# A two-layer decoder trunk on one core: one projection's banks, the order of the recurrence's output, late gating operands, and the final norm under the last product

## The chip, the core and the metric

The kernel runs on one core of a Trainium2 chip. The metric is the time of one execution on the device in microseconds (us). The core has a matmul engine (TensorE, PE in the profile), three engines for elementwise work (VectorE, DVE; ScalarE, ACT; GpSimd, POOL) and SyncE (SP), which here only starts DMAs. Each engine takes its own instructions in order and waits at semaphores for the others. PE writes its products into PSUM, which has eight banks of 128 x 512 f32. All else lies in SBUF.

## What is computed

512 tokens of width 1024 go through two layers; each adds to x half an FFN, a mixer, and half another FFN, all of normed x. The mixer of layer 0 is a recurrence, that of layer 1 a gated spatial mixer (gMLP). A final norm ends it.

```python
def rms_norm(x, g):
    y = xf * lax.rsqrt(jnp.mean(xf * xf, axis=-1, keepdims=True) + NORM_EPS)
    return (y * g.astype(jnp.float32)).astype(x.dtype)

def swiglu(x, w_in, w_out):                 # w_in 1024 x 5632, w_out 2816 x 1024
    g, u = jnp.split(x @ w_in, 2, axis=-1)
    return (jax.nn.silu(g) * u) @ w_out

def recurrent_mixer(...):
    y, r = jnp.split(x @ w_in, 2, axis=-1)
    y = jax.nn.gelu(y)
    r = causal_depthwise_conv(r, conv_w, conv_b)
    h = rg_lru(r, gate_a_w, gate_a_b, gate_x_w, gate_x_b, lam)
    return (y * h) @ w_out

def spatial_gating_mixer(...):
    u, v = jnp.split(jax.nn.gelu(x @ w_in), 2, axis=-1)
    v = rms_norm(v, v_norm)
    ...
    return (u * sg) @ w_out                 # sg: v mixed over positions, by head

for i in range(DEPTH):
    h = h + 0.5 * swiglu(rms_norm(h, ffn1_norm[i]), ffn1_w_in[i], ffn1_w_out[i])
    hn = rms_norm(h, mix_norm[i])
    ...
    h = h + m
    h = h + 0.5 * swiglu(rms_norm(h, ffn2_norm[i]), ffn2_w_in[i], ffn2_w_out[i])
return rms_norm(h, final_norm)
```

## The kernel before

**Steps.** The whole program is one list of steps (`subs`), each a block of weights of 256 x 512 and the matmuls that use it, mostly twelve of 128 x 512. The loop at the end of `trunk` goes through the list: for step i it issues what is hooked to i as "pre", then the splitting of the weights of step i + 3 (`SPLIT_AHEAD`), then the hooks "mid" and "rest", new loads, the matmuls of step i, and the hooks "end" and "late". `hook(n, phase, fn)` is how everything else (copies out of PSUM, transposes, norms, sums) gets its place. The order on every engine is so written out by hand.

**Splitting.** Each f32 operand is held as the sum of two fp32r parts. For a weight block ACT makes `whi` (line 96) and DVE makes `wlo` = raw - whi (line 87); for the left operand, `hi` and `lo`. A product takes three matmuls: hi with whi (line 360), lo with whi (line 361), hi with wlo (line 362). Four buffers each hold whi and wlo.

**Seven products.** `seven` computes a 2 x 2 block product of halves (tokens by columns, summed over two halves of the inner dimension) with seven products in place of eight, by Winograd's sums. The products are P1, P2, P5, P6, P3, P7, Q4, each over one or two groups (`cuts`, `ci` is the group). Their left operands are blocks A11, A12, A22, A21 of the left matrix and its sums S1 = A21 - A22, S2 = S1 - A11, S4, S3 (`s1`, `s2`, `s4`, `s3` on DVE); their right operands are weight blocks W11, W12, W21, W22 and sums of these. A weight sum comes about in one of two ways: an accumulating load on POOL's queue (`Raw.add`, line 136, "plus" or "then"), or a DVE add of two raw blocks (`Sub.add`, the group raw<-raw,raw of line 87). P6's operand is made in the second way, from P5's block and a tile of W22, which P3 then uses again. Results lie in PSUM under the names A (P1, then P6, P7, Q4 added to it), B (P2), C (P5, then P3), and Q (a bank of its own for Q4 in output products).

**Banks.** Six banks are for products (`bank`), two are aux banks (`aux`), in which PE transposes the left operands (tile e, line 264).

**The four places that the change touches.**
1. *First FFN chunk.* The first step list of all is a pair product (`pair_plain`, tile p, line 714) with four banks; `post` computes h = silu(p) * p with ACT and DVE (line 93), which frees its banks. Then a `chunk` follows through `seven`: P1 into A, P2 into B, P5 into C and so on; `p2` adds B to the copy c1 on DVE. h is transposed by `left_blocks` (tile e).
2. *The recurrence's output.* `recurrent` computes y in eight steps; the first three y are copied out of PSUM by DVE (`drain`, COPY y<-r), gelu follows on ACT, and DVE computes the scans and y * h, whose blocks are the left operands of the output product in `out_blocks`, in the order P1 P2 P5 of each group, then P6 P6 P3 P3 P7 P7 Q4 Q4.
3. *The norm before the spatial mixer* (`BlockNorm` with `plain`). x is transposed and multiplied by the gain; A21 is also split straight from PSUM (`direct`: per group twice ACT hi and DVE lo). Two transposes of the position weights (`tr_ws`, `take_ws`, tile wst) are hooked beside the mixer's first product.
4. *The final FFN's output and the final norm* (`FinalNorm`). Products in the usual order with Q4 last; for Q4 the first group's matmuls are held back and run with the second's (`joined`). Tokens lie in four tiles; tiles 0 and 1 get their last part from P3, tiles 2 and 3 from Q4. For each tile ACT squares and sums the two halves, ACT takes the root, DVE corrects the reciprocal by one Newton step (`newton`), and the two halves are multiplied by it and the gain on DVE and ACT and stored, one DMA on SP's queue and one on ACT's.

```python
def seven(block, cuts, left, w, posts, order=None, own=False, apart=False, joined=None):
    ...
    if fresh and ci == 0:
        for s in range(2):
            bk[name, s] = bank(name)[:, :w]
```

Of the kernel before, what the change touches and what calls it, by code (L numbers as in the profile page):

```python
# [13 lines left out]
P = 128  # L14
# [38 lines left out]
def trunk(ctx: ExitStack, tc: tile.TileContext, a: dict, out: bass.AP):  # L53
# [191 lines left out]
    class Group:  # L245
# [46 lines left out]

        def stage(self, n, name, src, gains=None, parts=True, where=None, direct=False):

            st = {}
            hook(n, "end", lambda: st.update(ps=self.turn(src, where)))
            first = name == "A21"
            hook(n + 1, "pre" if first else "mid", lambda: self.take(name, st["ps"], gains))
            if direct:
                hook(n + 1, "mid", lambda: self.direct(name, st["ps"], gains))  # L300
            hook(n + 1, "mid", st.clear)
            if parts:
                hook(n + 1, "mid", lambda: self.parts("S1" if first else name))
# [28 lines left out]

    def seven(block, cuts, left, w, posts, order=None, own=False, apart=False, joined=None):

# [7 lines left out]
        def mm_of(prod, ci):  # L342
# [102 lines left out]
    class BlockNorm:  # L445
# [102 lines left out]
    def out_blocks(w, k0, groups, scale, norm=None, order=None, own=False):  # L548
# [36 lines left out]

        def p3(s, ps):
            upd(s, 1, ps, scale)
            final(s, 1, "A12", s)
# [6 lines left out]
        def q4(s, ps):  # L595
            if hasattr(norm, "last"):
                norm.last(2 + s, ps, scale)
                return
            upd(2 + s, 0, ps, scale)
            final(2 + s, 0, "A21", s)  # L600

        at0 = len(subs)
# [39 lines left out]

    def chunk(w_in, f0, nt, group):

# [34 lines left out]
        def q4(s, ps):  # L679
# [4 lines left out]
            if s == 1:  # L684
                left_blocks(group, ht, 1)

        seven(in_block(w_in, lambda n: n * DFF + f0 * P, w), [[0, 1], [2, 3]], x_left(), w,
              dict(P1=p1, P2=p2, P5=p5, P6=p6, P3=p3, P7=p7, Q4=q4))

    def pair_plain(w_in, f0, group, first=False):  # L690
# [14 lines left out]
        def product(sub, half, left, h, between=None):  # L705

            sq = [(s, q) for q in range(2) for s in range(2)]
            for i, (s, q, m) in enumerate([(s, q, m) for m in range(3) for s, q in sq] if first and h else
                                          [(s, q, m) for q in range(2) for m in range(3) for s in range(2)] if first else
                                          [(s, q, m) for s, q in sorted(sq) for m in range(3)]):  # L710
                if i == 8 and between is not None:
# [4 lines left out]
                                 stop=left[2] == "1" and (h, q, m) == (1, 1, 2))  # L716

        def post(half):
            for s in range(2):
                ps, t = st[half, s], 2 * half + s  # L720
                s1, o = slot(name="s1")[:, :w], slot(name="h")[:, :w]
                act(s1, ps[:, :w], AF.Silu, scale=S.rt[:, t : t + 1])
                stt(o, ps[:, w:], S.rt[:, t : t + 1], s1, ALU.mult, ALU.mult)
# [31 lines left out]
    def ffn(w_in, w_out, norm):  # L755
        f0 = 0
        for i, sizes in enumerate(FF_PARTS):
            groups, p0 = [], f0
            for n in sizes:
# [11 lines left out]

    class FinalNorm:
        def __init__(self):
            self.gain, self.ms, self.r = {}, {}, {}

# [5 lines left out]

        def mean(self, t, n):

            junk = slot(name="junk")
            q = cp.tile([P, 1], F32, tag=f"ssq{t}{n}", name=f"ssq{t}{n}")
            act(junk, xt(t, n), AF.Square, accum_out=q)
            m = cp.tile([P, 1], F32, tag=f"ms{t}{n}", name=f"ms{t}{n}")
            ts(m, q, 1.0 / D, self.ms.get(t, EPS), ALU.mult, ALU.add)
            self.ms[t] = m

        def root(self, t):
            self.r[t] = tiny(1)
            act(self.r[t], self.ms[t], AF.Sqrt)

        def newton(self, t):
            r, m, c = self.r[t], self.ms[t], tiny(1)
# [8 lines left out]
        def store(self, t):  # L805

            o = xt(t, 0)
            stt(o, o, self.r[t], self.gain[0], ALU.mult, ALU.mult)
            act(xt(t, 1), xt(t, 1), AF.Copy, scale=self.r[t])
            for n, q in ((0, nc.sync), (1, nc.scalar)):  # L810
                q.dma_start(out=out[0, t * P : (t + 1) * P, n * 512 : (n + 1) * 512], in_=xt(t, n))

        def piece(self, t, n):
            at = now[0]
            if t < 2:
                hook(at + 1, "pre" if n == 1 else "mid", lambda: self.mean(t, n))
                if n == 1:
                    hook(at + 1, "mid", lambda: self.root(t))
                    hook(at + 2, "pre", lambda: self.newton(t))
                    hook(at + 2, "rest", lambda: self.grown(t, 1))  # L820
                    hook(at + 3, "rest", lambda: self.store(t))
            else:
                self.mean(t, n)
                hook(at + 1, "rest", lambda: self.grown(t, 1))

        def last(self, t, ps, scale):
            stt(xt(t, 0), ps, scale, xt(t, 0), ALU.mult, ALU.add)
            if t == 3:
                self.store(2)
            self.mean(t, 0)  # L830
            self.root(t)
            self.newton(t)
            if t == 3:
                self.store(3)


    def recurrent(w_in, w_out, norm):
# [83 lines left out]

        def drain(c):
            y = slot(name="y")
            nc.vector.tensor_copy(y, ym[c])
            ym[c] = y

        def gelu(c):
# [89 lines left out]
    def spatial(w_in, w_out, norm):  # L1017
# [256 lines left out]
    ffn(a["ffn2_w_in"][1], a["ffn2_w_out"][1], last)  # L1274
    hook(len(subs) - 24, "late", last.load)


# [153 lines left out]
```

## Time and profile before

| | |
|---|---|
| median of 3 runs | 1650.31 us (1649.54 to 1651.78) |
| the profiled execution's own time | 1652.41 us |
| its span in the trace | 1650.7 us, granted TensorE clock 0.992 |
| last matmul ends | 1637.40 us from the span's start |
| accumulating loads on POOL, issue to landing | medians 7.6 (ffn_w_in) and 8.0 us (ffn_w_out), 5.9 us (rec_w_out) |

Times below are counted from the start of the span. In the waits view a line names the waiting engine, tile and line, what released it, and the total, number and longest of such waits in us. In a timeline each row has start, duration, engine, line, operation and tiles, and in brackets the idle time before it with its releaser. Matmuls are pipelined: each takes 0.39 us by its row, but a 128 x 512 one starts 0.227 us after the one before it. The same holds on DVE and ACT in a smaller measure (a wlo takes 1.22 us and the next instruction starts 1.14 after it).

### The profile page before, as it was taken

The page shows a single profiled execution, that of the slowest core. Times are in us where ns is not written, and L with a number is a line of the kernel's source. Part 1 is how long each engine was busy: PE and PEld are TensorE (multiplying, and loading weights), DVE is VectorE, ACT ScalarE, POOL GpSimd, SP SyncE. Part 2 cuts the span into 40 slices and gives each one's busy share as a digit, 9 for nine tenths or more (in the row PEclk, how much of TensorE's full clock was granted, in tenths as well). Part 3 has the DMA queues.
Part 4 walks back from the last instruction along what each step waited for, and adds up shares of the span by engine and source line. Part 5 has one row for each costly group of instructions (what it writes and reads, how often), then busy time and mean ns, then how long its engine had stood idle before and what let it go on. Part 6 is the DMA issues. An engine that isn't in the chain of part 4 may idle for free.

```text
span 1650.7 us, 20821 instructions
## 1 busy us (share of the span) xinstructions
PE 1621.5 (98%) x7475; PEld 1336.7 (81%) x7475; DVE 1367.8 (83%) x1836; ACT 1032.8 (63%) x1498; POOL 210.7 (13%) x191
## 2 busy tenths in 40 slices
PE   8999999999999999999999999999999999999996
PEld 6788888888878888888888888888788888888885
DVE  6898898887898787978887978778866888879777
ACT  6656656657866656556775565566864865665655
POOL 1111111100000111111101111112100011121110
PEclk9999999999999999999999999999999999999999
DMA  5767876943363786866838768768753557696682
GB/s 212 161 170 173 204 170 163 212 132 96 101 168 86 175 199 160 212 170 159 207 86 181 187 172 209 167 161 225 183 158 90 152 120 186 166 211 166 158 205 77
DMA packets 160744, 271.97 MB, mean 165 GB/s; under 512 B 11280, under 2 KB 37504, under 8 KB 160640
## 3 DMA queue, kind: packets, MB, share of 16 engines
q1 hardware_dynamic: 113424, 181.95, 35.3%
q0 software_dynamic: 44992, 86.06, 31.3%
q10 hardware_dynamic: 2224, 2.63, 0.5%
q8 instruction: 59, 0.97, 0.2%
q14 instruction: 45, 0.37, 0.1%
HBM read 268.50 MB, written 2.10 MB: 164 GB/s over the span
## 4 chain that ended last, share of the span: by engine, by line
PE 88%; DVE 7%; ACT 3%; issue 1%; DMA 0%; SPq 0%; ACTq 0%; DVEq 0%
PE A L361 13%; PE A L360 13%; PE A L362 13%; PE C L361 7%; PE C L362 7%; PE C L360 7%; PE p L714 4%; PE B L360 3%; PE B L362 3%; PE B L361 3%; PE e L264 3%; DVE wlo L87 2%; PE Q L360 1%; PE Q L362 1%; PE Q L361 1%
## 5 line engine op out<-in xcount | busy, mean ns | idle before, releaser
L96 ACT ACTIVATE whi<-raw 128x1024 fp32r<-128x1024 f32 (+1 forms) x530 | 546.9, 1033 | 407.9 <-PE A L361 111.9
L87 DVE TENSOR_TENSOR wlo<-raw,whi 128x1024 fp32r<-128x1024 f32 (+1 forms) x531 | 631.2, 1191 | 198.8 <-ACT whi L96 197.7
L360 PE MATMUL A<-whi,hi 128*128 128x512 f32 x984 | 392.7, 399 | 0.8 <-DVE x L93 0.8
L361 PE MATMUL A<-whi,lo 128*128 128x512 f32 x984 | 385.5, 392 | 4.8 <-DVE lo L87 4.8
L362 PE MATMUL A<-wlo,hi 128*128 128x512 f32 x984 | 385.8, 392 | 0.0
L361 PEld LDWEIGHTS A<-whi,lo 128*128 128x128 f32 x984 | 186.0, 189 | 42.8 <-DVE lo L87 5.8
L362 PEld LDWEIGHTS A<-wlo,hi 128*128 128x128 f32 x984 | 185.6, 189 | 40.3
L360 PEld LDWEIGHTS A<-whi,hi 128*128 128x128 f32 x984 | 185.6, 189 | 38.2 <-ACT hi L96 1.6
L361 PE MATMUL C<-whi,lo 128*128 128x512 f32 x544 | 212.4, 390 | 1.4 <-DVE lo L87 1.2
L360 PE MATMUL C<-whi,hi 128*128 128x512 f32 x544 | 212.3, 390 | 0.0
L362 PE MATMUL C<-wlo,hi 128*128 128x512 f32 x544 | 211.8, 389 | 0.0
L136 POOL DMA_DIRECT2D raw<-in_ffn_w_in_dram x80 | 96.4, 1205 | 753.4 <-DVE raw L87 560.8
L136 POOL DMA_DIRECT2D raw<-in_ffn_w_out_dram x72 | 83.0, 1153 | 387.3 <-DVE wlo L87 153.5
L87 DVE TENSOR_TENSOR raw<-raw,raw 128x1024 f32<-128x1024 f32 (+1 forms) x110 | 131.9, 1199 | 0.5
L87 DVE TENSOR_TENSOR lo<-a,hi 128x512 fp32r<-128x512 f32 (+1 forms) x188 | 122.5, 658 | 3.9 <-ACT hi L96 3.4
L361 PEld LDWEIGHTS C<-whi,lo 128*128 128x128 f32 x544 | 102.1, 188 | 24.7 <-DVE lo L87 3.7
L96 ACT ACTIVATE hi<-a 128x512 fp32r<-128x512 f32 (+1 forms) x188 | 112.5, 600 | 14.3 <-DVE a L87 12.1
L362 PEld LDWEIGHTS C<-wlo,hi 128*128 128x128 f32 x544 | 102.1, 188 | 21.2
L360 PEld LDWEIGHTS C<-whi,hi 128*128 128x128 f32 x544 | 102.1, 188 | 21.0
L360 PE MATMUL B<-whi,hi 128*128 128x512 f32 x272 | 110.2, 405 | 5.3 <-DVE h L93 5.3
L96 ACT ACTIVATE c<-A 128x512 f32<-128x512 f32 x126 | 74.3, 595 | 57.6 <-PE A L362 57.1
L361 PE MATMUL B<-whi,lo 128*128 128x512 f32 x272 | 107.0, 393 | 0.0
(168 smaller groups left out, 2206.9 us busy)
## 6 DMA issues: line engine op xcount, KB each, us to landing
raw<-in_ffn_w_in_dram SPq DMA_DIRECT2D x160, 512.0 KB, 4.5
raw<-in_ffn_w_out_dram SPq DMA_DIRECT2D x100, 512.0 KB, 5.6
raw<-in_ffn_w_in_dram POOLq DMA_DIRECT2D x80, 512.0 KB, 7.6
raw<-in_ffn_w_out_dram POOLq DMA_DIRECT2D x60, 512.0 KB, 8.0
raw<-in_sg_w_in_dram SPq DMA_DIRECT2D x18, 512.0 KB, 5.3
raw<-in_rec_w_in_dram SPq DMA_DIRECT2D x16, 512.0 KB, 3.8
raw<-in_ffn_w_in_dram SPq DMA_DIRECT2D x30, 256.0 KB, 3.8
raw<-in_ffn_w_out_dram SPq DMA_DIRECT2D x20, 256.0 KB, 5.3
```

Source lines behind the costliest of these rows:

```text
L87: nc.vector.tensor_tensor(out=o, in0=x, in1=y, op=op)
L96: nc.scalar.activation(out=o, in_=x, func=f, **k)
L136: nc.gpsimd.dma_start(out=self.v, in_=src, accum_op=ALU.add)
L264: nc.tensor.transpose(ps[:, o : o + P], src(q, s), ident)
L360: nc.tensor.matmul(ps, zh, wh, start=fresh and i == 0, stop=False, **k)
L361: nc.tensor.matmul(ps, zl, wh, start=False, stop=False, **k)
L362: nc.tensor.matmul(ps, zh, wl, start=False, stop=end, **k)
L714: nc.tensor.matmul(bank_of(half, s), z, (sub.lo if m == 2 else sub.hi)[:, q, :], start=left[2] == "2" and (h, q, m) == (0, 0, 0), stop=lef ...
```

## The change

By place:

1. In the first FFN, the first chunk's B takes the two aux banks (`spare`). The pair's silu is hooked one step earlier and split from the rest of `post`; h's transposes are hooked two steps later (`left_blocks` with 4 for 2).
2. In the recurrence's output the order becomes P1 P5 P2 for each group, then P6 P3 for each, then P7 P7 Q4 Q4. The three copies of y are removed; gelu reads PSUM. Where P5 and P6 of a group are at least four steps apart (`far`), P6's weight sum is made by a second accumulating load onto P5's block, and P3 loads its own W22. By its distance this also holds for the first group in the spatial mixer's output. The sums s2, s4, s3 get other hooks.
3. In the plain norm `direct` of A21 runs five steps later, and the position weights' transposes and copies two steps later.
4. In the final FFN's output the order ends with P3, which is held back in the place of Q4, so that tiles 2 and 3 are finished first. `FinalNorm` is rewritten: half of the factor is put into the gain beforehand, the square's scale holds 1/1024, the root takes its bias from the other half's sum, the Newton step works on two tiles at once where it can, ACT's root table is loaded ten steps before the end, and the eight stores go out singly, seven on SP's queue and one on ACT's.

```diff
-        def stage(self, n, name, src, gains=None, parts=True, where=None, direct=False):
+        def stage(self, n, name, src, gains=None, parts=True, where=None, direct=0):
...
             if direct:
-                hook(n + 1, "mid", lambda: self.direct(name, st["ps"], gains))
-            hook(n + 1, "mid", st.clear)
+                hook(n + direct, "mid", lambda: self.direct(name, st["ps"], gains))
+            hook(n + max(direct, 1), "mid", st.clear)
...
-                        bk[name, s] = bank(name)[:, :w]
+                        bk[name, s] = (spare if name == "B" else bank)(name)[:, :w]
...
+        def far(ci):
+            return own and order.index(("P6", ci)) - order.index(("P5", ci)) >= 4
...
                 if own:
                     raw[11, ci] = new(0, 0, (0, 1))
+                    if far(ci):
+                        then = block(1, 1, cuts[ci])
...
+            elif prod == "P6" and far(ci):
+                r, then = raw[11, ci], block(1, 0, cuts[ci])
...
-                r = raw[22, ci]
+                r = new(1, 1) if far(ci) else raw[22, ci]
...
-                        self.plain if name == "A21" else name != "A22", direct=name == "A21")
+                        self.plain if name == "A21" else name != "A22",
+                        direct=0 if name != "A21" else 6 if self.plain else 1)
...
         def p3(s, ps):
+            if ends:
+                norm.last(s, ps, scale)
+                return
...
-                      "Q4" if hasattr(norm, "last") else None)
+                      "P3" if ends else None)
...
-                lead = 4 if isinstance(norm, TileNorm) and prod in ("P7", "Q4") else 3 if 1 in n else 2
+                lead = 6 if ends and prod == "P3" else 4 if isinstance(norm, TileNorm) and prod in ("P7", "Q4") else 3 if 1 in n else 2
...
+        def silu(half, s):
+            t = 2 * half + s
+            ht[t] = slot(name="s1")[:, :w]
+            act(ht[t], st[half, s][:, :w], AF.Silu, scale=S.rt[:, t : t + 1])
...
-            left_blocks(group, ht, half, 2)
+            left_blocks(group, ht, half, 4 if first else 2)
...
-                    end = (lambda: hook(at0 + 8, "rest", lambda: post(0))) if first else lambda: post(0)
+                    end = (lambda: (hook(at0 + 7, "rest", lambda: (silu(0, 0), silu(0, 1))),
+                                    hook(at0 + 8, "mid", lambda: post(0)))) if first else lambda: post(0)
...
-                    chunk(w_in, f0, n, groups[-1])
+                    chunk(w_in, f0, n, groups[-1], aux if len(subs) == 8 else bank)
...
+        ORDER = [(p, ci) for p in ("P1", "P2", "P5", "P6", "P7", "Q4", "P3") for ci in range(2)]
...
+        def root(self, t, n):
...
+            act(self.s[g][:, i : i + 1], self.q[g, n][:, i : i + 1], AF.Sqrt, bias=self.m[g][:, i : i + 1])
+
+        def newton(self, g, n, i):
+
+            r, q, m = self.s[g][:, i], self.q[g, n][:, i], self.m[g][:, i]
+            w = i.stop - i.start
+            v, c = tiny(w), tiny(w)
+            tt(v, q, m, ALU.add)
             nc.vector.reciprocal(out=r, in_=r)
-            stt(c, m, r, r, ALU.mult, ALU.mult)
-            ts(c, c, -0.5, 1.5, ALU.mult, ALU.add)
-            tt(r, r, c, ALU.mult)
+            if w == 1:
+                stt(c, r, v, r, ALU.mult, ALU.mult)
+            else:
+                tt(c, r, r, ALU.mult)
+                tt(c, c, v, ALU.mult)
+            stt(r, c, -3.0, r, ALU.add, ALU.mult)
...
+        def last(self, t, ps, scale):
+            stt(xt(t, 1), ps, scale, xt(t, 1), ALU.mult, ALU.add)
+            self.square(t, 1)
+            self.root(t, 1)
+            if t == 0:
+                self.both(2, 0)
+                self.both(3, 0)
+                self.scaled(2, 1)
+                self.scaled(3, 1)
             else:
...
+                self.both(0, 1)
+                self.scaled(0, 0)
+            self.newton(0, 1, slice(t, t + 1))
+            if t == 1:
+                self.both(1, 1)
+                self.scaled(1, 0, nc.scalar)
...
-        plan(1, "rest", (drain, 0), (sqrt, 0, 1, 2, 3, 4))
+        plan(1, "rest", (sqrt, 0, 1, 2, 3, 4))
         plan(1, "late", (scan, 0, 1))
-        plan(2, "rest", (exp_, 5, 6, 7), (drain, 1), (scan, 2, 3, 4), (oma2, 5, 6, 7))
-        plan(3, "rest", (drain, 2), (sqrt, 5, 6, 7))
+        plan(2, "rest", (exp_, 5, 6, 7), (scan, 2, 3, 4), (oma2, 5, 6, 7))
+        plan(3, "rest", (sqrt, 5, 6, 7))
...
-        sums(groups[0], y0 + 8)
-        sums(groups[1], y0 + 11)
+        for i, at in enumerate(((11, 12, 15), (13, 14, 16))):
+            for fn, n in zip((groups[i].s2, groups[i].s4, groups[i].s3), at):
+                hook(y0 + n, "pre", fn)
...
-        order = [(p, ci) for ci in range(2) for p in ("P1", "P2", "P5")]
-        order += [(p, ci) for p in ("P6", "P3", "P7", "Q4") for ci in range(2)]
+        order = [(p, ci) for ci in range(2) for p in ("P1", "P5", "P2")]
+        order += [(p, ci) for ci in range(2) for p in ("P6", "P3")]
+        order += [(p, ci) for p in ("P7", "Q4") for ci in range(2)]
...
-            hook(at0 + 6 + q, "end", lambda q=q: tr_ws(q))
-            hook(at0 + 7 + q, "mid", lambda q=q: take_ws(q))
+            hook(at0 + 8 + q, "end", lambda q=q: tr_ws(q))
+            hook(at0 + 9 + q, "mid", lambda q=q: take_ws(q))
...
+    hook(len(subs) - 16, "rest", last.halve)
+
+    hook(len(subs) - 10, "rest", lambda: act(tiny(1), vcol(0), AF.Sqrt))
```

More of the change, by code (lines that the diff above doesn't have):

```diff
@@ L331, in left_of, with seven @@
         return left
-    def seven(block, cuts, left, w, posts, order=None, own=False, apart=False, joined=None):
+    def seven(block, cuts, left, w, posts, order=None, own=False, apart=False, joined=None, spare=bank):
         bk, raw, held = {}, {}, []
@@ L640, in x_left, with chunk @@
         return left_of(lambda: S.z)
-    def chunk(w_in, f0, nt, group):
+    def chunk(w_in, f0, nt, group, spare=bank):
         w = nt * P
@@ L772, in trunk @@
     class FinalNorm:
+        ORDER = [(p, ci) for p in ("P1", "P2", "P5", "P6", "P7", "Q4", "P3") for ci in range(2)]
         def __init__(self):
-            self.gain, self.ms, self.r = {}, {}, {}
+            self.gain, self.q, self.m, self.s = {}, {}, {}, {}
         def load(self):
@@ L780, in load @@
                                     in_=a["final_norm"][n * 512 : (n + 1) * 512].partition_broadcast(P))
[L782 to L793, printed above, removed]
@@ L795, in newton, with halve, new, square @@
-        def newton(self, t):
-            r, m, c = self.r[t], self.ms[t], tiny(1)
-            nc.vector.reciprocal(out=r, in_=r)
-            stt(c, m, r, r, ALU.mult, ALU.mult)
-            ts(c, c, -0.5, 1.5, ALU.mult, ALU.add)
-            tt(r, r, c, ALU.mult)
+        def halve(self):
+            for n in range(2):
+                act(self.gain[n], self.gain[n], AF.Copy, scale=-0.5)
+        def new(self, name, w):
+            return cp.tile([P, w], F32, tag=nm(name), name=nm(name))
+        def square(self, t, n):
+            g = t // 2
+            if (g, n) not in self.q:
+                self.q[g, n] = self.new("fq", 2)
+            act(slot(name="junk"), xt(t, n), AF.Square, scale=1.0 / 32, accum_out=self.q[g, n][:, t % 2 : t % 2 + 1])
@@ new lines, in half @@
+        def half(self, g, n):
+            self.m[g] = self.new("fm", 2)
+            ts(self.m[g], self.q[g, n], EPS, None, ALU.add)
+        def root(self, t, n):
+            g, i = t // 2, t % 2
+            if g not in self.s:
+                self.s[g] = self.new("fs", 2)
+            act(self.s[g][:, i : i + 1], self.q[g, n][:, i : i + 1], AF.Sqrt, bias=self.m[g][:, i : i + 1])
[4 more added lines that the diff above has]
+            tt(v, q, m, ALU.add)
+            nc.vector.reciprocal(out=r, in_=r)
+            if w == 1:
[4 more added lines that the diff above has]
+            stt(r, c, -3.0, r, ALU.add, ALU.mult)
@@ L802, in grown, with r, both @@
+        def r(self, t):
+            return self.s[t // 2][:, t % 2 : t % 2 + 1]
         def grown(self, t, n):
             tt(xt(t, n), xt(t, n), self.gain[n], ALU.mult)
[L805 to L811, printed above, removed]
+        def both(self, t, n):
+            o = xt(t, n)
+            stt(o, o, self.r(t), self.gain[n], ALU.mult, ALU.mult)
+            self.store(t, n)
@@ L813, in piece, with scaled, store @@
+        def scaled(self, t, n, queue=None):
+            act(xt(t, n), xt(t, n), AF.Copy, scale=self.r(t))
+            self.store(t, n, queue)
+        def store(self, t, n, queue=None):
+            (queue or nc.sync).dma_start(out=out[0, t * P : (t + 1) * P, n * 512 : (n + 1) * 512], in_=xt(t, n))
         def piece(self, t, n):
             at = now[0]
[L815 to L821, printed above, removed]
-            else:
-                self.mean(t, n)
-                hook(at + 1, "rest", lambda: self.grown(t, 1))
@@ L826, in last @@
[L826 to L834, printed above, removed]
+            if (t, n) in ((1, 0), (3, 1)):
+                hook(at + 1, "mid", lambda: (self.square(t - 1, n), self.square(t, n)))
+                hook(at + 2, "pre", lambda: self.half(t // 2, n))
+                for i in range(2):
+                    hook(at + (2 if t == 1 else 1) + i, "rest", lambda i=i: self.grown(t - 1 + i, n))
+            elif t > 1 and n == 0:
+                self.square(t, 0)
+                self.root(t, 0)
+                if t == 3:
+                    hook(at + 1, "mid", lambda: self.newton(1, 0, slice(0, 2)))
```

20 lines of the change are left out of this document (8 added, 12 removed).

## The prediction, made before the changed kernel was run

> **What bounds the kernel now.** I read the page's busy shares first, then the chain that ended last, then the waits of PE, then the timelines around each wait.
>
> ```profile
> PE 1621.5 (98%) x7475; PEld 1336.7 (81%) x7475; DVE 1367.8 (83%) x1836; ACT 1032.8 (63%) x1498; POOL 210.7 (13%) x191
> ...
> PE 88%; DVE 7%; ACT 3%; issue 1%; DMA 0%; SPq 0%; ACTq 0%; DVEq 0%
> ```
>
> PE is busy 98% of the span and is most of the chain, so only two things can move the end: time in which PE stands still or runs slowly, and what follows its last matmul. The number of matmuls doesn't change. The waits of PE show where it stands:
>
> ```profile
> PE B L360 <- DVE h L93: 5.3, 1, 5.3
> PE A L361 <- DVE lo L87: 4.8, 2, 2.5
> PE warm L1314 <- DVE warm L1309: 1.3, 1, 1.3
> PE C L361 <- DVE lo L87: 1.2, 2, 1.0
> PE A L360 <- DVE x L93: 0.8, 1, 0.8
> ```
>
> (total, times, longest, in us.) Asked by windows, the 5.3 lies near 44, in the first FFN (place 1); the 1.0, the 0.8 and an A wait of 2.4 at 467 to 474, in the recurrence's output (place 2); the A wait of 2.5 at 1183 to 1186, in the spatial mixer's input (place 3). The diff touches these three and the end (place 4). Idle is not all of the price:
>
> ```profile
> 38.21 0.39 PE L362 MATMUL A<-wlo,hi 128*128 128x512 f32 x1
> 43.86 0.76 PE L360 MATMUL B<-whi,hi 128*128 128x512 f32 x1 [5.26 <-DVE h L93]
> 44.42 0.63 PE L361 MATMUL B<-whi,lo 128*128 128x512 f32 x1
> 44.85 0.63 PE L362 MATMUL B<-wlo,hi 128*128 128x512 f32 x1
> ...
> 48.63 0.40 PE L362 MATMUL B<-wlo,hi 128*128 128x512 f32 x1
> 48.87 0.38 PE L264 MATMUL e<-ident,h 128*128 128x128 f32 x2
> ```
>
> Elsewhere matmuls start every 0.227 us, twelve (one step) in 2.72; here the next eleven start every 0.43, so the wait costs 5.3 and 2.2 more. The same follows the waits of 2.37 (nine slow) and 2.48 (eleven), not those of 0.76 and 0.96. All PE time above 0.227 per matmul is 35 us of the span, some 20 of it at places 1 to 3.
>
> **The change, place by place.** I re-added each engine's list in its changed order with the durations of the same operations here: DVE's wlo 1.14 (start to next start), lo or 512-wide add 0.60, raw add 1.14, x update 0.60 to 0.64; ACT's whi 0.95, hi 0.52, table load 1.28.
>
> **Place 1.** B moves to the two aux banks, so it needn't wait for h to free bank p. It starts at 38.44 and then waits for operands: its wlo ends at 39.24 (0.4 idle), that of its second step at 42.71 (0.7), that of C's first step at 46.97 (1.5). C's first step ends at 49.3, at 0.227 per matmul, against 54.9 before. But next on PE's queue stand the transposes of h (tile e, two steps later than before), which write an aux bank, and B now holds both until DVE has added it to c1. DVE's list there, which stays:
>
> ```profile
> 53.49 1.22 DVE L87 TENSOR_TENSOR wlo<-raw,whi 128x1024 fp32r<-128x1024 f32 x1
> 54.62 0.69 DVE L87 TENSOR_TENSOR lo<-s,hi 128x512 fp32r<-128x512 f32 x1
> 55.22 0.42 DVE L87 TENSOR_TENSOR lo<-a,hi 128x256 fp32r<-128x256 f32 x1
> 55.56 1.28 DVE L87 TENSOR_TENSOR c<-c,B 128x512 f32<-128x512 f32 x2
> ```
>
> From 38 to 58 DVE is without a gap, and its order ahead of c<-c,B is unchanged except for the 0.34 of the lo<-a, which goes behind it. So the first c<-c,B runs 55.2 to 55.9, and PE waits 49.3 to 55.9: 6.6 idle, then eleven slow matmuls. Behind the waiting transpose stand C's second step, then P6 and P3. C's second step ends at 56.2 + 2.72 + 2.2 = 61.1, P6 and P3 (48 matmuls and four transposes) at 72.6; before, P3 ended at 69.5. **Place 1 costs 3.1.** Bounds: 0.9 if no matmul is slow, 3.9 if fifteen are; were the transposes not held, DVE's lo at 55.3 would be needed by P6's second matmul, and the place would gain 3.3. ACT's earlier silus and table load end at 40.1, the whi behind them at 41.2, still before DVE asks at 41.5: no cost, and each us that they were late would be one us on DVE's gapless list.
>
> **Place 2.** Between 430 and 490 DVE is busy 58.8 of 60 us (the windows view), and PE waits for its lo's. The edit takes three y copies (0.60 each; one lay in idle time) and two raw adds (1.14 each) off this list, and moves the sums s2, s4, s3 behind the lo's that PE needs first. Re-added, PE stands 0.3 at P5's second group (lo done 464.3), 0.7 at P3's first (473.2), 0.4 at P6's second (476.7), all under the 0.96 after which no slow matmuls came. P3's second step ends at 482.4 against 487.64: **gain 5.2**, of 6.5 that the waits and their slow matmuls cost here. Bounds: 3 (only the DVE work taken off between the first and last wait) and 6.5 (all). What pays for the adds: three accumulating loads more on POOL. The first starts at 457, behind P5's split, and P6's split asks at 463; the second 461.9, asked for at 470. Their landing is bounded by rec_w_out's own rows on POOL, 5.9 in the median (4.6 to 8.4 with sg_w_out's), and by the slowest of all 171, 11.2. I take 5.9, the same matrix in the same stage: just hidden. Without the y copies, a bank comes free when ACT's gelu has read it: done at 441.2, asked for at 442.0, hidden by 0.8. In the spatial mixer's output one raw add goes too, where PE doesn't wait: 0; its accumulate has 11 us.
>
> **Place 3.** The A21 hi/lo pairs (two ACT, two DVE per group, which alternate and wait for each other: DVE's rows show 0.54 idle between) go five steps later, and the wst transposes two.
>
> ```profile
> 1185.96 0.80 PE L361 MATMUL A<-whi,lo 128*128 128x512 f32 x1 [2.48 <-DVE lo L87]
> ```
>
> This wait and its eleven slow matmuls go (P6 gets its lo at 1182.98, when it asks). What is late next: P3's first step, whose hi and lo stand behind the moved pairs (1.4 idle, until 1190); wst (0.35); P3's second (2.0, until 1195); P7's first (0.6). Re-added, Q4 ends at 1209.4 against 1211.38: **gain 2.0**. Bounds: 4 if ACT and DVE pass the pairs without alternating idle, and a loss of 2.6 if both new idles bring eleven slow matmuls (2 x 2.3).
> Whether 1.4 and 2.0 us of idle do that, no row says: 0.96 didn't, 2.37 did. I take no, as nearer to 0.96 for the one, undecided for the other.
> The Trainium skill, page "TensorE: Matmul & The Clock Gate", section "Part 1: The HAM clock gate", has the half-rate clock come after an idle window of about 3.4 us; the trace shows it after 2.37 already, so its figure doesn't hold here. By that figure the sum would stay, and the whole chance of the clock rival below would go to the forecast.
>
> **Place 4.** The last matmul ends at 1637.40, the span at 1650.72: 13.3 us, which go so:
>
> ```profile
> 1639.92 0.68 DVE L93 SCALAR_TENSOR_TENSOR x<-Q,x 128x512 f32<-128x512 f32 x1
> ...
> 1642.60 0.68 DVE L93 SCALAR_TENSOR_TENSOR x<-Q,x 128x512 f32<-128x512 f32 x1
> ...
> 1645.92 0.75 DVE L93 SCALAR_TENSOR_TENSOR x<-x,ti,fg 128x512 f32<-128x512 f32 x1
> ```
>
> After it the last stores start at 1646.7, land by 1649.5, and 1.2 more end the span. In the changed order the second tokens' normalisation (before: two x updates, two gain products and two 0.71 products on DVE ahead of x<-Q) runs beside the last 24 matmuls, and each remaining tail has two tiny operations of 0.2 fewer. Up to the last step DVE is full from 1614, so PE stands 0.2 and 0.8 more and ends at 1637.6. DVE then works in order: its Newton step waits for ACT's root of the third tile until 1637.1, the first x<-C (due 1635.1) follows, two gain products to 1639.0, Newton to 1639.9, the second x<-C to 1640.5; root, Newton and the last product to 1643.0. Store 2.9 (as 1646.67 to 1649.5), end 1.2: 1647.1. **Gain 3.5.** Bounds: 2, if ACT is late with the root by 1.5; 5.9, if DVE isn't behind and takes the first x<-C when PE has it. The gain's halving (two ACT products) and the early table load lie in idle of ACT (three idles of 1.1 and one of 2.1 from 1616 to 1627): 0, or 1.28 without that cover. Six stores more on SP's queue start one behind the other; the last two have the same distance as before.
>
> **Sum:** +3.1 - 5.2 - 2.0 - 3.5 = -7.6. The profiled span of 1650.7 becomes 1643.1, its execution 1652.41 becomes 1644.8; that execution is 2.1 above the median 1650.31, so the median becomes **1642.7**.
>
> **Rivals.**
> - *The transposes aren't held* at place 1 (DVE comes to c<-c,B before 53): the loss of 3.1 becomes the gain of 3.3, 1636.3. For it: the wait moved is the largest one. Against: DVE's gapless list.
> - *The clock falls at place 3.* Two idles of 1.4 and 2.0 within 5 us bring slow matmuls: 4.6 more, 1647.3. For it: 2.37 was enough.
> - *The tail isn't held by DVE* at place 4: 5.9 instead of 3.5, 1640.3. Against: DVE's full list from 1614.
> - *Slower: accumulating loads late* at place 2. POOL takes its queue in order; an accumulate held behind another one's wait starts late, and P6's split waits with DVE's whole list behind it. Each us past 463 is one us, and past 2.4 of them 2.3 once more. At the slowest landing seen, 11.2, place 2 turns from -5.2 to +2.3 (5.2 idle, 2.3 slow): 1650.2, no change; a landing 3.4 us later yet (by a late start, or 14.6 from the start) makes it 1653.6, and from there it is slower by over 0.2%. Against: no row lands so late.
> - *Nothing but the new bank wait is felt:* DVE's list bounds places 2 to 4 as before, 1653.4.
>
> **How the numbers follow.** Forecast 0.56; transposes not held 0.09; clock 0.14; tail free 0.10; accumulates late 0.07; only the bank wait 0.04. The range 1637 to 1650 leaves out the first rival's 1636.3 and what ends above 1650, some 0.18. About 0.2% (3.3 us: below 1647.0, above 1653.6) is what a measurement of this kernel tells from no change: faster gets the forecast, the first and the third rival and a fifth of the clock's, 0.78; same the rest of the clock's and part of the last two, 0.14; slower 0.08.
>
> **What would show it.** Place 1: in PE's waits a transpose e waiting some 6.6 for DVE c near 50 to 56, slow matmuls after it, P3 ending near 72.6. Place 2: no wait over 1 us between 440 and 490, no accumulate landing after P6's split asks. Place 3: the 2.48 gone, two waits of 1.4 and 2.0 at C near 1189 and 1194, clock 0.9 or more there. Place 4: the last x update some 3 us after the last matmul, and some 9.5 instead of 13.3 us from there to the end. A landing of an accumulate past 8 us, slow matmuls after idles below 2 us, or transposes that don't wait would each prove me wrong by the rival's price.

## The result, and the profile after

The changed kernel took 1654.86 us in the median of nine runs (1653.1 to 1657.46), the kernel before 1650.04 (1649.28 to 1651.78): a ratio of 1.0028, 95% interval 1.0018 to 1.0038. Timed a second time, beside the experiments, it was 1.0011 (1.0002 to 1.0020). It is slower by 0.1 to 0.3%; the forecast was 1642.7 and faster.

The profiled execution of the changed kernel took 1653.5 us, with a span of 1651.7. It is one of the quickest of its runs, while that of before (1652.41) is slower than all nine of its runs. So the two spans, 1.0 us apart, understate the difference; the span of a second trace of the changed kernel is 1653.7. What the traces do well is to say where. The table below takes the start of the same matmul in PE's list (its 300th and so on) from one trace each, and gives the time between such points in us. Each place lies within the stretch that names it; place 4's runs to the end of the span.

| stretch of PE's list | before | changed | changed, 2nd trace | forecast against before |
|---|---|---|---|---|
| to 300 (place 1) | 76.35 | 79.55 | 80.46 | +3.1 |
| 300 to 1500 | 265.57 | 265.60 | 265.58 | 0 |
| 1500 to 2400 (place 2) | 184.35 | 184.04 | 185.48 | -5.2 |
| 2400 to 5000 | 571.47 | 571.48 | 571.50 | 0 |
| 5000 to 5800 (place 3) | 171.90 | 170.53 | 170.18 | -2.0 |
| 5800 to 7200 | 306.32 | 306.19 | 306.20 | 0 |
| 7200 to the end (place 4) | 74.76 | 74.32 | 74.32 | -3.5 |

The stretches of the four places hold all but 0.1 us of the difference between the first two traces. These are the changed kernel's busy shares and its chain:

```profile
PE 1621.3 (98%) x7475; PEld 1334.7 (81%) x7475; DVE 1361.2 (82%) x1821; ACT 1033.6 (63%) x1501; POOL 214.1 (13%) x194
...
PE 87%; DVE 6%; ACT 4%; issue 1%; DMA 1%; SPq 0%; ACTq 0%; DVEq 0%
```

DVE has 6.6 us less to do, and it bought nothing: DMA has entered the chain with 1%. PE's waits in the changed kernel say why:

```profile
PE e L264 <- DVE c L87: 6.3, 1, 6.3
PE C L362 <- ACT hi L96: 4.4, 3, 2.6
PE A L362 <- DVE x L93: 4.4, 1, 4.4
PE C L363 <- DVE lo L87: 1.5, 4, 0.8
```

The B wait of 5.3 and the A waits for lo are gone but for 0.2, as meant. In their place stand three others of over 2 us, one at each of places 1, 2 and 4.

**Place 1**, the changed kernel's PE timeline (tile e is the transposes of h):

```profile
49.49 0.40 PE L364 MATMUL C<-wlo,hi 128*128 128x512 f32 x1
56.22 0.69 PE L264 MATMUL e<-ident,h 128*128 128x128 f32 x2 [6.33 <-DVE c L87]
56.56 0.78 PE L362 MATMUL C<-whi,hi 128*128 128x512 f32 x1
57.13 0.63 PE L363 MATMUL C<-whi,lo 128*128 128x512 f32 x1
57.56 0.63 PE L364 MATMUL C<-wlo,hi 128*128 128x512 f32 x1
```

The transposes of h wait for DVE's c<-c,B to give an aux bank back, and the next matmuls start 0.43 apart.

**Place 2.** ACT's timeline first, then PE's:

```profile
468.28 0.62 ACT L96 ACTIVATE hi<-a 128x512 fp32r<-128x512 f32 x1
476.84 1.06 ACT L96 ACTIVATE whi<-raw 128x1024 fp32r<-128x1024 f32 x1 [7.94 <-DMA raw<-in_rec_w_out_dram]
477.80 0.61 ACT L96 ACTIVATE hi<-a 128x512 fp32r<-128x512 f32 x1
```

```profile
475.49 0.39 PE L364 MATMUL A<-wlo,hi 128*128 128x512 f32 x1
478.47 0.50 PE L362 MATMUL C<-whi,hi 128*128 128x512 f32 x1 [2.59 <-ACT hi L96]
479.81 0.65 PE L363 MATMUL C<-whi,lo 128*128 128x512 f32 x1 [0.84 <-DVE lo L87]
480.26 0.63 PE L364 MATMUL C<-wlo,hi 128*128 128x512 f32 x1
```

PE's wait names ACT's hi (of P3's first group). That hi was not late by itself: it stood in ACT's queue behind the whi of P6's second group, and this whi waited 7.9 us for an accumulating load. Read a wait on an engine back to what that engine waited for.

**Place 4**, PE and then DVE:

```profile
1621.53 0.39 PE L364 MATMUL A<-wlo,hi 128*128 128x512 f32 x1
1626.31 0.47 PE L362 MATMUL A<-whi,hi 128*128 128x512 f32 x1 [4.39 <-DVE x L93]
1626.62 0.40 PE L363 MATMUL A<-whi,lo 128*128 128x512 f32 x1
1626.85 0.60 PE L364 MATMUL A<-wlo,hi 128*128 128x512 f32 x1
```

```profile
1624.27 0.69 DVE L87 TENSOR_TENSOR lo<-s,hi 128x512 fp32r<-128x512 f32 x1
1624.88 0.69 DVE L87 TENSOR_TENSOR lo<-a,hi 128x512 fp32r<-128x512 f32 x1
1625.48 1.28 DVE L93 SCALAR_TENSOR_TENSOR x<-A,x 128x512 f32<-128x512 f32 x2
```

P6's last matmul starts at 1621.5, and P7, which adds to the same banks A, may start only when DVE has read A for P6's update of x. DVE comes to that at 1625.5. In the kernel before, P6's last matmul and the same read stand so:

```profile
1620.10 0.39 PE L362 MATMUL A<-wlo,hi 128*128 128x512 f32 x1
...
1621.34 1.28 DVE L93 SCALAR_TENSOR_TENSOR x<-A,x 128x512 f32<-128x512 f32 x2
```

There the 24 matmuls of P3 came next on PE, and P7 started at 1625.8, long after the read. The read itself also came sooner: 1.2 us after the start of P6's last matmul, against 3.9 in the changed kernel, where a gain product and the lo's of the products that now come next stand ahead of it in DVE's list. The last matmul ends at 1644.5 (before: 1637.4), and from there to the end of the span it is 7.2 us (before: 13.3).

### The profile page after: what moved, and what is told of

Its sections match the earlier page's. It is cut to its first block, busy times and chain, and to the rows that moved or that the text cites. A ratio compares the mean times of both kernels' runs of the same rounds, so it can differ in the third digit from the quotient of the medians.

```text
span 1651.7 us, 20816 instructions
## 1 busy us (share of the span) xinstructions
PE 1621.3 (98%) x7475; PEld 1334.7 (81%) x7475; DVE 1361.2 (82%) x1821; ACT 1033.6 (63%) x1501; POOL 214.1 (13%) x194
## 4 chain that ended last, share of the span: by engine, by line
PE 87%; DVE 6%; ACT 4%; issue 1%; DMA 1%; SPq 0%; ACTq 0%; DVEq 0%
PE A L362 13%; PE A L363 13%; PE A L364 13%; PE C L363 7%; PE C L364 7%; PE C L362 7%; PE p L727 4%; PE e L264 3%; PE B L362 3%; PE B L364 3%; PE B L363 3%; DVE wlo L87 2%; PE Q L364 1%; PE Q L362 1%; PE Q L363 1%
## 5 line engine op out<-in xcount | busy, mean ns | idle before, releaser
L87 DVE TENSOR_TENSOR raw<-raw,raw 128x1024 f32<-128x1024 f32 (+1 forms) x107 | 128.2, 1199 | 0.5
L364 PE MATMUL B<-wlo,hi 128*128 128x512 f32 x272 | 106.5, 391 | 0.6 <-DVE wlo L87 0.6
```

The costliest lines, as they stand in the source:

```text
L87: nc.vector.tensor_tensor(out=o, in0=x, in1=y, op=op)
L364: nc.tensor.matmul(ps, zh, wl, start=False, stop=end, **k)
```

## The experiments

Each run is timed beside the kernel before on the same chip. The median of before itself was 1651.5 us beside e1 to e4, 1652.1 beside e5 to e8 and 1650.6 beside e9 to e11, so the ratios to it are to be compared, not the microseconds. The changed kernel itself stood at 1.0028 and 1.0011. Times of places are those of the table's stretches, from one trace of each run.

**e1_place1_back.** Place 1 as before.

```diff
-            left_blocks(group, ht, half, 4 if first else 2)
+            left_blocks(group, ht, half, 2)
-                    end = (lambda: (hook(at0 + 7, "rest", lambda: (silu(0, 0), silu(0, 1))),
-                                    hook(at0 + 8, "mid", lambda: post(0)))) if first else lambda: post(0)
+                    end = (lambda: hook(at0 + 8, "rest", lambda: post(0))) if first else lambda: post(0)
-                    chunk(w_in, f0, n, groups[-1], aux if len(subs) == 8 else bank)
+                    chunk(w_in, f0, n, groups[-1])
```

> The changed kernel with place 1 as before (B in the banks of the products, silu and transposes at their old steps). Theory, from the trace: the aux-bank wait costs 3.2 us net, so this is 3.2 us below the changed kernel: about 1651.7 us where before has 1650.0; in its trace the 6.3 us wait of the transposes is gone, the 5.3 us wait of B is back, and the later places look as in the changed kernel. Rival: what place 1 loses is given back at a later wait; then the time stays at 1654.9, within 1 us.

Measured: 1651.84 us, ratio 1.0000 (0.9991 to 1.0009). The first stretch took 76.66, so undoing place 1 takes out 2.9 of its 3.2; the other places were within 0.9 us of the changed kernel's two traces (185.10, 170.14, 75.19). The trace bears the theory out; the ratio came out 0.1% below the 1.0010 that it gave.

**e2_h_in_banks.** The first half's transposes of h in product banks.

```diff
-            g.stage(n, "A11", src(0, 0))
-            g.stage(n + 1, "A12", src(1, 0))
+            g.stage(n, "A11", src(0, 0), where=where)
+            g.stage(n + 1, "A12", src(1, 0), where=where)
...
-            left_blocks(group, ht, half, 4 if first else 2)
+            left_blocks(group, ht, half, 4 if first else 2, bank if first and half == 0 else None)
```

> The changed kernel, but the first half's transposes of h at place 1 go into the product banks that the pair product has left, not into the aux banks that B holds. Theory: PE then waits under 1 us there, the 6.3 us and the ten or so slow matmuls go, and the time is some 6.5 us below the changed kernel (3.2 lost and 3.3 to gain): about 1648.4 us. Rival (VectorE's gapless list binds anyway, so the wait only moves to P6): under 3 us gained, 1652 or more.

Measured: 1650.59 us, ratio 0.9993 (0.9984 to 1.0002). The first stretch fell to 75.19, that is 4.4 below the changed kernel and 1.2 below before, not 6.5: the second half's transposes still waited 1.9 for the same c<-c,B, and two waits for a wlo of 1.2 and 1.0 stayed. At place 2 the wait for ACT's hi grew to 4.4 in this trace. A part theory, a part rival.

**e3_accum_from_5.** Accumulating loads only from five steps on.

```diff
-            return own and order.index(("P6", ci)) - order.index(("P5", ci)) >= 4
+            return own and order.index(("P6", ci)) - order.index(("P5", ci)) >= 5
```

> The changed kernel, but accumulating loads replace the raw adds only where P5 and P6 are five steps apart: the recurrence's second group and the spatial mixer's first group add on VectorE again. Theory: at place 2 ScalarE's whi of P6's second group stood behind an accumulating load that took 9.8 us, and the hi of P3's first group behind that whi; with this load gone the 2.6 and 0.8 us waits and the eight slow matmuls go, VectorE has 1.1 us more to do: 2 to 5 us below the changed kernel, 1650 to 1653 us. Rival (VectorE's list binds place 2, as before): the wait comes back at a lo of P3 or P6, under 1 us gained.

Measured: 1651.19 us, ratio 0.9996 (0.9987 to 1.0004). Place 2 took 181.80, which is 2.2 below the changed kernel and 2.5 below before. No wait over 0.7 us was left there. So the load was the cause; DVE's raw add gives part of it back. The edit also takes the added load out of the spatial mixer's output, which the trace doesn't show to matter (170.13 and 306.30 in the two stretches there).

**e4_p3_between.** P3's first group between P6 and P7.

```diff
-        ORDER = [(p, ci) for p in ("P1", "P2", "P5", "P6", "P7", "Q4", "P3") for ci in range(2)]
+        ORDER = [(p, ci) for p in ("P1", "P2", "P5", "P6") for ci in range(2)] + [("P3", 0)]
+        ORDER += [(p, ci) for p in ("P7", "Q4") for ci in range(2)] + [("P3", 1)]
...
-                      "P3" if ends else None)
+                      None)
...
-                lead = 6 if ends and prod == "P3" else 4 if
+                lead = 6 if ends and (prod, ci) == ("P3", 1) else 4 if
```

> The changed kernel, but in the last output product the first group of P3 runs between P6 and P7, and only its second group is last. Theory: P7 adds to A, which VectorE must have read for P6's update; with 12 matmuls (2.7 us) between them the 4.4 us wait falls to 1.7 or less and no matmuls are slow after it, which takes 2.7 to 5 us from the end of the last matmul; the second tokens' norm has half the cover, 1 to 2 us more after the last matmul: 1651 to 1654 us, 1 to 4 below the changed kernel. Rival (VectorE's list sets the end whatever PE does): within 1 us of the changed kernel.

Measured: 1650.68 us, ratio 0.9998 (0.9989 to 1.0006). PE's timeline of this kernel:

```profile
1625.01 0.39 PE L364 MATMUL C<-wlo,hi 128*128 128x512 f32 x1
1626.24 0.47 PE L362 MATMUL A<-whi,hi 128*128 128x512 f32 x1 [0.84 <-DVE x L93]
1626.55 0.40 PE L363 MATMUL A<-whi,lo 128*128 128x512 f32 x1
1626.78 0.39 PE L364 MATMUL A<-wlo,hi 128*128 128x512 f32 x1
```

The same wait is 0.84 and no matmul is slow after it. From the last matmul to the end it is 9.5 us in place of 7.2; place 4 took 71.63, 2.7 below the changed kernel and 3.1 below before. The theory held, but for a tail that grew by 2.3 instead of 1 to 2. With half of P3's matmuls in between, the read of A at its late place in DVE's list is nearly hidden; moving it forward in that list was not tried.

**e5_after_again.** The changed kernel, unedited.

> The changed kernel as it is, timed again beside the others. The traces put it 1.0 us above before (place 1 +3.2, place 2 -0.3, place 3 -1.4, place 4 -0.5), the medians of the first measurement 4.8. Theory: the sum of the places is the real difference, and the rest lies in the few us by which executions of either kernel differ: the ratio comes out at 1.0005 to 1.0015. Rival: there is a cost outside the four places, in most executions but not in the traced one: 1.0025 to 1.0035 again, and a trace that shows a wait or slow matmuls elsewhere.

Measured: 1653.88 us, ratio 1.0011 (1.0002 to 1.0020). Its trace is the 2nd trace of the table above: the same waits, with that at place 2 at 4.1 instead of 2.6, and nothing elsewhere. So a good part of the first measurement's 4.8 us is what runs differ by; what of it is not is open.

**e6_three_fixes.** e2 (with the second half's transposes one step later still), e3 and e4 together.

```diff
-            left_blocks(group, ht, half, 4 if first else 2)
+            left_blocks(group, ht, half, 4 + half if first else 2, bank if first and half == 0 else None)
```

> The changed kernel with three mends: h's first transposes at place 1 in the product banks and those of its second half one step later; accumulating loads only from five steps on (place 2); P3's first group between P6 and P7 (place 4). If the places add, as the theory has it, the traces of the single mends give, against before, -1.2 and 2 more for the transposes' remaining wait at place 1, -2.5 at place 2, -1.6 at place 3, -3.1 at place 4: 1640 to 1643 us where before has 1650 to 1651.5. Rival: VectorE's lists bind, so that a wait taken away at one place comes back at the next: 1646 or more.

Measured: 1643.69 us, ratio 0.9947 (0.9935 to 0.9960). Its trace has 75.21, 181.79, 170.31 and 71.66 at the four places; 1.1, 2.6, 1.6 and 3.1 below before, 8.4 in sum. The places add. Not one matmul after 30 us is slow. Only place 1 is short of the forecast (1.1 in place of 3.2): there DVE's list does bind, with waits of 1.2, 1.0 and twice 0.6 to 1.0 along it.

**e7_p7_sum_later.** P7's accumulating load two steps later.

```diff
-                pending.append((now[0] + 2, self))
+                pending.append((now[0] + self.delay, self))
+                pending.sort(key=lambda p: p[0])
...
                 r = new(0, 1, (1, 1)) if own else raw[12, ci]
+                if far(ci) and far(1):
+                    r.delay = 4
```

> The changed kernel, but at place 2 the accumulating load for P7's sum is issued two steps later, so that it is not in flight beside the one that P6's second group waits for. Theory (accumulating loads that run beside each other slow each other: 5.8 us alone, 9.8 to 12.3 with two or three in flight): that load lands within 7 us of its start, ScalarE's wait for it falls from 7.9 to under 4 us, PE's 2.6 us wait and the eight slow matmuls go; 3 to 5 us below the changed kernel. Rival (the load is slow by itself or by the plain loads beside it): it lands 9 us or more after its start and the wait stays.

Measured: 1650.68 us, ratio 0.9992 (0.9983 to 1.0001). Place 2 took 180.63: 3.4 below the changed kernel, 3.7 below before, PE's waits there at most 0.6. ACT's timeline:

```profile
468.51 0.62 ACT L96 ACTIVATE hi<-a 128x512 fp32r<-128x512 f32 x1
471.12 1.06 ACT L96 ACTIVATE whi<-raw 128x1024 fp32r<-128x1024 f32 x1 [1.99 <-DMA raw<-in_rec_w_out_dram]
472.10 0.61 ACT L96 ACTIVATE hi<-a 128x512 fp32r<-128x512 f32 x1
```

The traces' start and landing of each accumulating load of this stage (us):

| kernel | start to landing (time taken) |
|---|---|
| before | 450.3 to 456.7 (6.5); 458.6 to 464.5 (6.0); 471.0 to 477.0 (5.9); 474.0 to 479.9 (5.9) |
| changed | 454.6 to 460.5 (5.9); 455.3 to 464.4 (9.0); 466.3 to 473.5 (7.3); **467.0 to 476.7 (9.8)**; 469.6 to 480.2 (10.6); 479.5 to 485.3 (5.8) |
| e7 | 454.9 to 460.6 (5.8); 455.6 to 465.0 (9.4); **465.1 to 471.0 (5.9)**; 466.5 to 476.0 (9.5); 469.8 to 479.6 (9.8); 476.3 to 482.9 (6.6) |

Bold is the load that P6's second group waits for. In e7 P7's load still goes out close behind it, so "not in flight beside" was put too strongly; being first in line is what counted. A lone load takes 5.8 to 6.5 in this table, and loads that start close behind one another land 3.2 to 5 us after each other (2.6 to 5.5 over all the traces), always in the order of their start. P7's load cost the other one its start too: POOL issued it first, at 466.3, and the bold one 0.7 later at 467.0, though what that one waits for itself, DVE's wlo of P5's second group, was done at 464.6. In e7 it went out 0.3 after that wlo.

**e8_place4_back.** `FinalNorm`, the last product's order and its posts as before (Q4 last and held back, gain, roots and stores of before).

```diff
-        if ends:
-            order = norm.ORDER
...
-                      "P3" if ends else None)
+                      "Q4" if ends else None)
```

> The changed kernel with the last product's order and the final norm as before. Theory: the gain after the last matmul (13.3 to 7.2 us) was eaten by the 4.4 us wait of P7 for VectorE's reading of A and the slow matmuls behind it; so place 4 as a whole is worth nothing, and this is within 1 us of the changed kernel, its last matmul 6.6 us earlier and its tail 6 us longer. Rival (place 4 is where the change loses): 2 us or more below the changed kernel.

Measured: 1654.46 us, ratio 1.0016 (1.0007 to 1.0024), the changed kernel's time. Place 4 took 74.77 (changed 74.32), its last matmul to the end 13.3 us. The theory held: all that was won after the last matmul was lost before it.

**e9_mends_p7.** e6 with e7's edit in place of e3's.

> The kernel of the three mends, but at place 2 all accumulating loads stay and P7's goes out two steps later instead. Theory: POOL's accumulating loads are served one after the other, about 3.3 us each with 5.8 for a lone one, so the load first in line lands in time; place 2 takes 1.2 us less than in the three mends by the traces (180.6 against 181.8), 1 to 2 us below it: about 0.994 of before. Rival (what the raw add costs VectorE there is hidden): the same as the three mends, 0.9947, within 0.5 us.

Measured: 1642.77 us, ratio 0.9948 (0.9934 to 0.9962). Its trace has 180.65 at place 2, 1.1 less than e6, but the times don't tell the two apart. Both are 0.5% below before, and the changed kernel stood above before each time.

**e10_place3_back.** Place 3 as before.

```diff
-                        direct=0 if name != "A21" else 6 if self.plain else 1)
+                        direct=int(name == "A21"))
-            hook(at0 + 8 + q, "end", lambda q=q: tr_ws(q))
-            hook(at0 + 9 + q, "mid", lambda q=q: take_ws(q))
+            hook(at0 + 6 + q, "end", lambda q=q: tr_ws(q))
+            hook(at0 + 7 + q, "mid", lambda q=q: take_ws(q))
```

> The changed kernel with place 3 as before. Theory, from the traces: the move takes out a 2.5 us wait with about ten slow matmuls and brings three waits of 0.8 to 1.0 us with none, 1.4 to 1.8 us net; this is that much slower than the changed kernel, 1.002 of before. Rival: the shift is regained by slack before the position products, no difference.

Measured: 1653.99 us, ratio 1.0017 (1.0008 to 1.0026): not told apart from the changed kernel. The trace contradicts the theory's price: place 3 took 169.20, less than the 170.53 with the edit.

```profile
1187.15 0.49 PE L362 MATMUL A<-whi,hi 128*128 128x512 f32 x1
1190.12 0.50 PE L363 MATMUL A<-whi,lo 128*128 128x512 f32 x1 [2.48 <-DVE lo L87]
1190.46 0.39 PE L364 MATMUL A<-wlo,hi 128*128 128x512 f32 x1
1190.69 0.40 PE L362 MATMUL A<-whi,hi 128*128 128x512 f32 x1
```

It is the same 2.48 wait as in the trace of before, but no matmul is slow after it, and the stretch takes 2.7 less than there. So the edit trades one wait of 2.5 for smaller ones of nearly the same sum. Against the execution of before in which that wait brought slow matmuls (171.90) it gains 1.0 to 1.8, by the eleven traces that have it (170.13 to 170.86); against this one it loses 0.9 to 1.7. How often the wait brings them was not tried.

**e11_y_copies_back.** e9 with the three y copies on DVE again.

```diff
-        plan(1, "rest", (sqrt, 0, 1, 2, 3, 4))
+        plan(1, "rest", (drain, 0), (sqrt, 0, 1, 2, 3, 4))
```

(and the copies 1 and 2 in the plans 2 and 3)

> The kernel of the run before last in this call, with the three copies of y out of PSUM put back on VectorE. Theory of the prediction: two of the three copies (0.6 us each) lie on VectorE's full list, so this is about 1.2 us slower than without them. Rival (the list has slack there now): no difference, within 0.5 us.

Measured: 1643.03 us, ratio 0.9950 (0.9937 to 0.9963), no difference that the times show. The trace has 181.25 at place 2 against 180.65: 0.6, half of what was expected.

## Why the prediction was wrong, step by step

- **What bounds the kernel: right.** Time moved only where PE's waits moved; the three stretches between the places agree within 0.13 us in the table's three traces.
- **Place 1, +3.1: right.** Measured +3.2, the wait 6.3 (6.6 forecast), the transpose's start 56.2. The price of the other case, a gain of 3.3, was too high: with the first half's transposes in product banks it was 1.1 to 1.9 (e2, e6, e9, e11).
- **Place 2, -5.2: wrong** (-0.3, and +1.1 in the second trace). The step that failed is "I take 5.9, the same matrix in the same stage: just hidden". The 5.9 was of loads that started 3 us or more apart, mostly 8 to 12. The change puts two more into the same 25 us, with P7's ahead of the one that mattered: that one started some 2 us late and took 9.8, and landed at 476.7, where in e7 it took 5.9 and landed at 471.0. I had listed this as the rival "accumulating loads late" with a chance of 0.07, for P6's first group and by the rows' spread, and had not counted who stands ahead in the queue. The rest of the step stood: with that load first in line (e7), place 2 gains 3.7, within the bounds 3 to 6.5. (The lower figure 4.6 for the loads of these two matrices stands in no row: they took 5.7 to 8.4.)
- **Place 3, -2.0: near in size in the trace (-1.4), but by luck.** The waits came out at 0.8, 0.2, 1.0, 0.2 and 0.2, less than the 1.4 and 2.0 forecast, with no slow matmuls. But the sum took the slow matmuls behind the old wait as certain, and the gain is nothing but their price: in e10 they don't come, and the old order is 0.9 to 1.7 quicker than the new one.
- **Place 4, -3.5: wrong** (-0.4). The tail fell by more than I said, from 13.3 to 7.2. The step that failed is "PE stands 0.2 and 0.8 more and ends at 1637.6". Moving P3 to the end takes its 24 matmuls, 5.4 us, from between P6 and P7. They were the cover under which DVE read A; without them P7 waits 4.4 and some nine matmuls are slow. I counted what moved to the end and not what the moved matmuls had covered, nor that DVE's list would come to that read 2.7 later after P6 than before. e4, which leaves half of the cover, gains 3.1.
- **Sum.** With the two failed steps and place 1's hold mended, e6 and e9 measured 1643.7 and 1642.8, near the 1642.7 forecast for the change as it stood; in part by chance, as place 1 there gains 1.1 and 1.9 instead of losing 3.1. The rival nearest to the measured time, *nothing but the new bank wait is felt* with 1653.4, was not borne out: places 2 and 4 gained nothing not because DVE's list bound them as before, but because each traded its old price for a new wait that e7 and e4 take away.

## What to carry to other kernels

When a product is moved, ask what it stood between: a block of matmuls that separates a product from the next one into the same bank is the time in which that bank is read. A DMA's duration from a row holds for its place in its queue; when loads are added to a queue, list who goes out ahead, and price the one that is waited for from the end of that line. On an engine that works in order, a late operand also holds what stands behind it, so PE's wait can name an engine that did nothing wrong.

## What the runs showed of the hardware

Slow matmuls start 0.43 us after one another in place of 0.227. In the eleven traces here and the two of before and after, and after their first 30 us, they came behind every idle of PE of 2.4 us and more but one, and behind none of 1.9 us or less (two waits a matmul apart counted as one). They were not equally many: behind the same 2.48 us ten and none, behind the same 4.4 us from five to twelve. So one wait can cost up to 2.8 us more in one execution than in the next (that of 2.48, before against e10), and a price of it from a single trace is uncertain by that. The Trainium skill, page "TensorE: Matmul & The Clock Gate", section "Part 1: The HAM clock gate", says that the monitor's window runs freely, so that the number of slow matmuls depends on where in it work begins; the spread here agrees. Its idle window of about 3.4 us does not: 2.48 us was enough at place 3 of before, where PE's waits view shows no other wait from 1175 to 1215. The 2.37 us at place 2, from which the prediction argued, is the weaker case, as an idle of 0.76 stands one matmul ahead of it; and seven matmuls, not nine, start 0.43 apart behind it.

The changed kernel's runs spread over 4.4 and 2.8 us (nine and eleven runs), those of e6 and e9, whose traces show no slow matmul after 30 us, over 1.3 and 1.0 (five each). The granted clock on record for each run goes with its time: of the 74 timed runs of before beside the experiments, the 39 at 0.994 took 1649.5 to 1652.1 us and the 35 at 0.991 to 0.993 took 1651.2 to 1654.4; the traced one stood at 0.992. So the runs of one kernel differ in how long its matmuls are slow. That these waits are where they differ is likely from this, and not shown.
